# A softmax on one core: the fifth and the sixth chunk are loaded the first time in halves

## The chip, the core and the metric

The kernel runs on one core of a Trainium2 chip. The metric is the device time of one execution in microseconds (us). Three runs of the kernel before took 2488.24 to 2488.63 us, with a median of 2488.45.

## The reference

The kernel computes a softmax over the last axis of float32 logits, 16 x 256 rows of 32768 values each, with a temperature of 1.0:

```python
scaled = logits / temperature
scaled = scaled - scaled.max(axis=-1, keepdims=True)
exp_scaled = np.exp(scaled)
return exp_scaled / exp_scaled.sum(axis=-1, keepdims=True)
```

Every value is read once and written once: 536.87 MB in and 536.87 MB out.

## The kernel before

**Tiling.** The 4096 rows of 32768 values are seen as 8192 half rows of 16384. A group is 128 half rows, one on each partition, that is 64 whole rows; G = 64 groups in all. A group is cut into two chunks of 8192 columns (`_CW`): 128 partitions x 32 KB, 4 MB. So there are 128 chunks. SBUF has six slots of one chunk each (`_BUFS`, 192 KB on every partition); group g has the slots 2g mod 6 and 2g + 1 mod 6 (`slots`). Work is in place: the load, the exponential, the scaling and the store of a chunk all use its slot.

**One group** (class `Half`). For each of its chunks DVE waits for the load and takes the negated maximum of the chunk (`tensor_reduce`, L123); ACT then writes the exponential of the chunk with that maximum as its bias, and sums it as it goes (`activation`, L168). When both are done, DVE swaps the maxima and sums between the two half rows of a row (L134), takes the common maximum (L138), ACT takes the correction factors (L179), DVE sums with them (L142), inverts (L153) and scales each chunk (`tensor_scalar`, L157). Each scaled chunk is stored.

**Who issues what.** SP issues all loads on its own queue (q1 in the profile), and ACT issues the stores (q10) of all groups but the last three, whose stores SP issues behind the last loads (L103). The order of everything is written out by hand; no scheduler is in between.

- SP first issues the loads of the first three groups into the six free slots (L216 to L218). Group 0 is loaded with `load_edge` (L94): each chunk in two halves of 4096 columns (`_EDGE`, 16 KB per partition, 2 MB) with a semaphore each. Groups 1 and 2 are loaded with `load` (L89): one transfer of 4 MB a chunk. The chunks of group 2 are the fifth and the sixth; they go to slots 4 and 5.
- SP then loops 20 times over the six slots (L219 to L222): it waits until the store out of a slot has landed (`st[b]`) and loads the next chunk into it. The last group, number 63, is again loaded in halves (L223 to L225).
- DVE runs group 0 (L228), then a loop of 20 turns of three groups (L229 to L231), whose waits count on the loop's register: `ld[b]` must have reached 16 for each load into slot b, since a transfer adds 16 when it has landed. Groups 61 to 63 follow (L232). ACT has the same structure (L236 to L245).
- Group 63 alone is computed and stored in pieces of 4096 columns; group 0 is loaded in halves and computed in whole chunks.

The counts that DVE waits for stand in these lines:

```python
    def turn(q, i):
        b = slots(q + 1)
        return Half(f"q{q}", (q + 1) % _SETS, b, _CW, lambda c, s: [(ld[b[c]], i * 16)], i)
```

Of the kernel before, what the change touches and what calls it, by code (L numbers as in the profile page):

```python
# [8 lines left out]
_CW = 8192  # L9
_BUFS = 6  # L10
_EDGE = 4096
_SETS = 3
# [13 lines left out]
def kernel(  # L26
# [20 lines left out]
    x = xf.rearrange("n (h v) -> (n h) v", h=2)  # L47
# [20 lines left out]
    ld = [nc.alloc_semaphore(f"ld{b}") for b in range(_BUFS)]  # L68
# [9 lines left out]
    sp, dve, act = nc.sync, nc.vector, nc.scalar  # L78

    def spans(step):  # L80
        return [(s, step) for s in range(0, _CW, step)]

    def xcols(b, s, n):
        return X[:, b * _CW + s : b * _CW + s + n]

    def rows(g):
        return bass.ds(g * P, P)
# [6 lines left out]
    def load_edge(g, c, b):  # L94
        for s, n in spans(_EDGE):
# [3 lines left out]
                out=xcols(b, s, n), in_=x[rows(g), c * _CW + s : c * _CW + s + n]  # L99
            ).then_inc(sem, 16)  # L100

    def store(q, g, c, b, s, n):
        q.dma_start(  # L103
            out=o[rows(g), c * _CW + s : c * _CW + s + n], in_=xcols(b, s, n)
        ).then_inc(st[b], 16)

    class Half:
# [79 lines left out]
        def stores(self, q, g):  # L187
            for k, (c, s, w) in enumerate(self.pieces):
                q.wait_ge(site(self.tag, "sc", k), self.n)
                store(q, g, c, self.slots[c], s, w)  # L190

    def slots(g):
        return [2 * g % _BUFS, (2 * g + 1) % _BUFS]

    def fine(g):
        return lambda c, s: [(edge[g, c, s], 16)]

    def coarse(n16):
        return lambda c, s: [(ld[b], n16)] if s == 0 else []


    def first():
        return Half("f", 0, slots(0), _CW, lambda c, s: [(edge[0, c, p], 16) for p, _ in spans(_EDGE)], 1)

    def turn(q, i):
        b = slots(q + 1)
        return Half(f"q{q}", (q + 1) % _SETS, b, _CW, lambda c, s: [(ld[b[c]], i * 16)], i)

    def last(g):
        b = slots(g)  # L210
        if g == G - 1:
            return Half("l2", g % _SETS, b, _EDGE, fine(g), 1)
        return Half(f"l{g}", g % _SETS, b, _CW, lambda c, s: [(ld[b[c]], (g // _SETS + (b[c] > 1)) * 16)], 1)


    for g in range(_SETS):  # L216
        for c in range(2):
            (load_edge if g == 0 else load)(g, c, slots(g)[c])  # L218
    with sp.Fori(1, turns + 1) as i:  # L219
        for b in range(_BUFS):  # L220
            sp.wait_ge(st[b], i * 16)
# [7 lines left out]
    with dve.Fori(1, turns + 1) as i:  # L229
        for q in range(_SETS):  # L230
            turn(q, i).vector()  # L231
    for g in range(G - 3, G):  # L232
        last(g).vector()


    f = first()  # L236
    f.scalar()
    f.stores(act, 0)
    with act.Fori(1, turns + 1) as i:
        for q in range(_SETS):  # L240
            h = turn(q, i)
            h.scalar()
            h.stores(act, i * _SETS + (q + 1 - _SETS))
    for g in range(G - 3, G):
        last(g).scalar()  # L245


    for g in range(G - 3, G):
        last(g).stores(sp, g)
# [41 lines left out]
```

## Time and profile before

| What | us |
|---|---|
| median of three runs | 2488.45 (2488.24 to 2488.63) |
| the profiled execution | 2488.27 |
| its span, from the first to the last instruction | 2486.5 |
| DVE busy | 1724.6 (69%) |
| ACT busy | 944.5 (38%) |
| POOL busy | 0.2 |

The DMA issues of the page (line, queue, count, KB each, median us from issue to landing):

```profile
xs<-in_logits_dram SPq DMA_DIRECT2D x124, 4096.0 KB, 26.5
out_dram<-xs ACTq DMA_DIRECT2D x122, 4096.0 KB, 48.3
xs<-in_logits_dram SPq DMA_DIRECT2D x8, 2048.0 KB, 16.1
out_dram<-xs SPq DMA_DIRECT2D x4, 4096.0 KB, 33.7
out_dram<-xs SPq DMA_DIRECT2D x4, 2048.0 KB, 21.9
```

The page is read like this. DVE is the vector engine, ACT the scalar engine, SP the engine that only issues here; L90 is line 90 of the kernel. "Busy" counts an engine's own instructions, not the issuing of DMAs. All DMA queues share the core's 16 DMA engines, and a transfer over 128 partitions is spread over all 16. `xs` is the tensor of the six slots. A transfer's time from issue to landing holds its wait in the queue as well as its bytes, and it lands when its last byte has arrived and the semaphore tells so. Times inside the execution are counted from the start of the span. The times to landing of single transfers, which are used below, come from the trace asked for one line in a narrow window; the time of a landing is the time of issue plus that.

### The profile page before, as it was taken

Reading aid. Unit: us, or ns where it says so; the run is one execution under the profiler, and the core shown is the slowest. Engines: PE = TensorE matmul, PEld = TensorE weight load, DVE = VectorE, ACT = ScalarE, POOL = GpSimd, SP = SyncE. Lnnn points to the kernel's source line nnn. Section 1 sums busy time; section 2 is a strip of 40 time slices with the busy share of each in tenths; the row PEclk is TensorE's granted clock in tenths of the full one; section 3 lists DMA queues with packets and bytes.
Section 4 is the critical chain, followed back from the end, with each engine's and each line's share of the span. In section 5 each row is a group of like instructions: output and inputs, shape, how many; then the busy total and the mean of one; then the engine's idle time right before and its main releaser. Section 6 shows DMA issues by size and latency. Waiting matters only on the chain.

```text
span 2486.5 us, 2019 instructions
## 1 busy us (share of the span) xinstructions
DVE 1724.6 (69%) x644; ACT 944.5 (38%) x325; POOL 0.2 (0%) x4
## 2 busy tenths in 40 slices
DVE  6777767767677676676766767667676676766764
ACT  3444333343333433434334343343433434334342
POOL 0000000000000000000000000000000000000000
DMA  9999999999999999999999999999999999999999
GB/s 413 430 435 433 430 438 431 430 438 431 432 436 431 436 432 431 438 430 432 437 430 434 435 430 438 431 430 438 431 432 436 431 436 432 431 438 431 430 437 399
DMA packets 37730, 1073.77 MB, mean 432 GB/s; under 512 B 4192, under 2 KB 4192, under 8 KB 4192
## 3 DMA queue, kind: packets, MB, share of 16 engines
q1 hardware_dynamic: 20160, 562.05, 52.4%
q10 hardware_dynamic: 17568, 511.71, 47.7%
q14 instruction: 2, 0.02, 0.0%
HBM read 536.87 MB, written 536.87 MB: 432 GB/s over the span
## 4 chain that ended last, share of the span: by engine, by line
DMA 58%; DVE 18%; another core or an unknown queue 14%; ACT 8%; issue 1%; SPq 0%; ACTq 0%; DVEq 0%
DMA out_dram<-xs 37%; DMA xs<-in_logits_dram 21%; DVE t L123 11%; ACT xs L168 7%; DVE xs L157 6%; SPq L90 0%; ACT ee L179 0%; DVE t L134 0%; DVE row L153 0%; DVE row L138 0%; DVE junk L142 0%; ACTq L103 0%; SPq L98 0%; DVEq L133 0%
## 5 line engine op out<-in xcount | busy, mean ns | idle before, releaser
L168 ACT ACTIVATE xs<-xs,t 128x8192 f32<-128x8192 f32 (+1 forms) x130 | 912.1, 7016 | 1468.4 <-DVE t L123 1468.4
L123 DVE TENSOR_REDUCE t<-xs 128x1 f32<-128x8192 f32 (+1 forms) x130 | 1110.8, 8551 | 234.0 <-DMA xs<-in_logits_dram 234.0
L157 DVE TENSOR_SCALAR xs<-xs,ee,row 128x8192 f32<-128x8192 f32 (+1 forms) x130 | 576.5, 4478 | 2.3
L134 DVE LOAD_MASK_SELECT t<-t x64 | 0.9, 14 | 470.3 <-ACT xs L168 470.3
L179 ACT ACTIVATE ee<-t,row 128x4 f32<-128x4 f32 x64 | 19.0, 298 | 35.9 <-DVE row L138 35.9
L142 DVE CUSTOM_DVE_ANT_1 junk<-ee,t 128x4 f32<-128x4 f32 x64 | 10.4, 163 | 23.3 <-ACT ee L179 23.3
L168 ACT ACTIVATION_READ_ACCUMULATOR xs<-xs,t 128x1 f32 x130 | 24.3, 187 | 0.0
L153 DVE RECIPROCAL row<-row 128x1 f32<-128x1 f32 x64 | 10.5, 164 | 2.2
L138 DVE TENSOR_REDUCE row<-t 128x1 f32<-128x4 f32 x64 | 10.1, 157 | 2.2
L134 DVE STREAM_SHUFFLE t<-t 128x4 f32<-128x4 f32 x64 | 10.2, 160 | 0.6
L142 DVE DVE_READ_ACCUMULATOR2_ANT row<- 128x1 f32 x64 | 5.3, 82 | 0.0
L168 ACT ACT_TABLE_LOAD x1 | 1.3, 1283 | 0.9 <-SPq L54 0.9
L272 POOL MEMSET const-bfloat16-1.0<- 128x1 bf16 x1 | 0.1, 102 | 0.0
L272 POOL MEMSET const-uint8-127<- 128x1 uint8 x1 | 0.1, 101 | 0.0
L272 POOL MEMSET const-float32-0.0<- 128x1 f32 x1 | 0.1, 99 | 0.2 <-issue 0.2
L272 POOL MEMSET const-float32-1.0<- 128x1 f32 x1 | 0.1, 98 | 0.0
## 6 DMA issues: line engine op xcount, KB each, us to landing
xs<-in_logits_dram SPq DMA_DIRECT2D x124, 4096.0 KB, 26.5
out_dram<-xs ACTq DMA_DIRECT2D x122, 4096.0 KB, 48.3
xs<-in_logits_dram SPq DMA_DIRECT2D x8, 2048.0 KB, 16.1
out_dram<-xs SPq DMA_DIRECT2D x4, 4096.0 KB, 33.7
out_dram<-xs SPq DMA_DIRECT2D x4, 2048.0 KB, 21.9
```

Of the source, the lines that this page charges most:

```text
L123: m = dve.tensor_reduce(out=t[:, k : k + 1], in_=xcols(self.slots[c], s, w), axis=X_, op=A.max, negate=True)
L134: dve.stream_shuffle(out=t[:, 2 * K : 4 * K], in_=t[:, 0 : 2 * K], mask=swap).then_inc(site(tag, "sh"), 1)
L138: dve.tensor_reduce(out=r[:, 0:1], in_=tv[:, :, 0, :], axis=XY, op=A.min).then_inc(site(tag, "mx"), 1)
L142: dve.tensor_tensor_reduce(out=j[:, 0 : 2 * K].rearrange("p (a k) -> p a k", a=2), in0=e[:, 0 : 2 * K].rearrange("p (a k) -> p a k", a=2), ...
L153: dve.reciprocal(out=r[:, 2:3], in_=r[:, 1:2]).then_inc(site(tag, "rc"), 1)
L157: dve.tensor_scalar(out=xs, in0=xs, scalar1=e[:, k : k + 1], scalar2=r[:, 2:3], op0=A.mult, op1=A.mult).then_inc(site(tag, "sc", k), 1)
L168: a = act.activation(out=xs, in_=xs, func=Exp, bias=t[:, k : k + 1], scale=inv_t, accum_out=t[:, K + k : K + k + 1],)
L179: act.activation(out=e[:, 0 : 2 * K].rearrange("p (a k) -> p a k", a=2), in_=tv[:, :, 0, :], func=Exp, bias=r[:, 0:1], scale=-1.0,).then_i ...
L272: nc = _bacc.Bacc("TRN2", target_bir_lowering=False, num_devices=1)
```

## The change

Group 2's two chunks are loaded with a new function, `load_halves`, in two transfers of 4096 columns (16 KB per partition) each. Both halves of a chunk add 16 to the same semaphore `ld[b]`, so slots 4 and 5 now count one transfer more than their chunks, and `landed16` gives the count that DVE waits for: both halves of the first chunk, then one more for each later one. DVE's reduces, their order and all other transfers are the same. An unused function, `coarse`, goes.

```diff
+    def load_halves(g, c, b):
+        for s, n in spans(_EDGE):
+            sp.dma_start(
+                out=xcols(b, s, n), in_=x[rows(g), c * _CW + s : c * _CW + s + n]
+            ).then_inc(ld[b], 16)
+
+
+    def landed16(b, n):
+        return (n + 1) * 16 if b // 2 == _SETS - 1 else n * 16
...
-    def coarse(n16):
-        return lambda c, s: [(ld[b], n16)] if s == 0 else []
-
...
     def turn(q, i):
         b = slots(q + 1)
-        return Half(f"q{q}", (q + 1) % _SETS, b, _CW, lambda c, s: [(ld[b[c]], i * 16)], i)
+        return Half(f"q{q}", (q + 1) % _SETS, b, _CW, lambda c, s: [(ld[b[c]], landed16(b[c], i))], i)
...
-        return Half(f"l{g}", g % _SETS, b, _CW, lambda c, s: [(ld[b[c]], (g // _SETS + (b[c] > 1)) * 16)], 1)
+        return Half(f"l{g}", g % _SETS, b, _CW, lambda c, s: [(ld[b[c]], landed16(b[c], g // _SETS + (b[c] > 1)))], 1)
...
     for g in range(_SETS):
         for c in range(2):
-            (load_edge if g == 0 else load)(g, c, slots(g)[c])
+            (load_edge if g == 0 else load_halves if g == _SETS - 1 else load)(g, c, slots(g)[c])
```

## The prediction

> **What bounds the kernel now.** I read the page's slices and queue rows first, to see whether any engine has idle time that an edit could give back or use up.
>
> ```profile
> DVE  6777767767677676676766767667676676766764
> DMA  9999999999999999999999999999999999999999
> ...
> q1 hardware_dynamic: 20160, 562.05, 52.4%
> q10 hardware_dynamic: 17568, 511.71, 47.7%
> ```
>
> DVE, the busiest engine, works in six to seven tenths of a slice; the 16 DMA engines work in all of them. The packets of the loads' queue (q1) and of ACT's store queue (q10) together fill 100.1% of the span: the transfers follow each other without a gap. Next the same by stretch (columns: length, busy time and count of DVE, ACT, POOL, PE clock, DMA share, GB/s), for the opening, the loop and the last 21.5 us:
>
> ```profile
> 50.00:110.00 60.00, 44.23 (x19) 29.45 (x10) 0.00 (x0) 1.00 0.99 428
> ...
> 400.00:2300.00 1900.00, 1320.44 (x490) 721.97 (x246) 0.00 (x0) 1.00 1.00 433
> ...
> 2465.00:2486.50 21.50, 0.00 (x0) 0.00 (x0) 0.00 (x0) 1.00 0.81 347
> ```
>
> 428 to 433 GB/s at a share of 0.99 to 1.00 in opening and loop; only the very end falls off. The chain of waits gives the price of a transfer: in the loop it repeats a piece each 116.29 us (load issues at 281.54 and 397.83), in which six chunks are loaded and six stored: 116.29 / 12 = **9.69 us for one 4 MB transfer**. 128 loads and 128 stores make 256 x 9.69 = 2480.9 us of the span of 2486.5. The remaining 5.6 are 0.95 to the first issue, 2.3 until its bytes flow (below), 1.2 after the last landing, and about 1.1 that I do not split. So the end is set by bytes in line at the DMA engines, and an edit moves the time only if it makes these engines idle, lets them begin earlier, or makes transfers dearer.
>
> Last, what the engines wait for, and the end of the chain:
>
> ```profile
> DVE t L123 <- DMA xs<-in_logits_dram: 234.0, 58, 13.1
> ```
>
> ```profile
> 2374.95 26.52 DMA xs<-in_logits_dram
> ...
> 2401.50 8.70 DVE t L123
> ...
> 2450.18 9.38 DVE xs L157 x4
> ```
>
> DVE waits for loads 58 times, 234.0 us: in the loop the compute follows the transfers. At the end, the last DVE work starts at 2450.18 and the span goes on to 2486.5 on stores alone.
>
> **The change, part by part.** The profiled execution took 2488.27 us, its span 2486.5, so 1.8 lie around it; the median of the runs is 2488.45, 0.18 more. I add the steps to the profiled time and give the sum against the median.
>
> 1. *Dearer transfers.* The fifth and sixth chunk are 4 transfers instead of 2. The price stands in the opening, where L98 loads halves back to back. Issue times 0.95 and 2.34 with 7.2 and 20.5 us to landing put the first half at 8.15 and the fourth at 22.8: three halves in 14.65, 4.88 each, 9.77 for a chunk. The third and fourth chunk (L90, issued 2.90 and 3.41, landing after 29.6 and 38.8) land 9.7 apart. A split chunk thus costs 0.07 to 0.08 more; twice, **+0.15 us**, all on the path, since the DMA line has no gap. The four half stores at the end agree: from 2470.7 to 2485.3, 4.87 each.
>
>    The other bound: the first half needs 7.2 us to land where one in line takes 4.88, so 2.3 us of a transfer are startup. Shown for both added transfers this is +4.6. I take 0.15, because the added halves are queued at about 4 us and start behind four transfers, as halves two to four of the opening do. 4.6 stays as the range's upper end; no row shows a split chunk coming out cheaper than a whole one.
>
>    The Trainium skill (DMA: Bandwidth & Descriptors, section Anatomy of one DMA) charges each transfer a fixed cost of about 2.0 us on GpSimd's path, which speaks against this change: two more would make an estimate of +4.0. The 4.88 us spacing disagrees for transfers in line; the measurement decides.
>
> 2. *SP's issues.* Two more issues of 0.33 to 0.50 us each (row of L90) put SP's loop about 0.9 us later. SP then waits for the first store, which lands at 68.4 (44.7 + 23.7); the loop is entered near 6. Cost 0; without that cover it would be 0.9, once. Nothing else stands in SP's queue there.
>
> 3. *The waits.* DVE still reduces whole chunks after both halves have landed, so no work begins sooner. In its loop the order of instructions shows one register instruction more (for the count of slots 4 and 5), 20 times. The existing one takes 54 ns (L229), 1.1 us in all, and its sequencer does it beside a TENSOR_SCALAR of 4.5 us. Cost 0; uncovered it would still have to exceed the 3.9 us that DVE waits for loads in each half.
>
> 4. *The share of the two queues in the opening.* This is what really moves. Today the fifth chunk lands at 56.3 (3.95 + 52.4), 14.1 after the fourth (42.2), 4.4 more than 9.7: the first store took those 4.4, so by equal turns sharing began at 47.5. From there each load takes 19.4. How a 16 KB load packet shares with a 32 KB store packet is seen at the end, where L98's first half (issued 2394.2, landing after 18.2, at 2412.4) starts at 2401.5, when the load ahead of it lands (2375.0 + 26.5), beside the last ACT store, which lands at 2410.5 (2350.3 + 60.2). Equal bytes would give it 4.5 of its 4.85 us by then and a landing at 2410.9; equal packets give it a third, 3.0, and 2410.5 + 1.85 = 2412.4. It landed at 2412.4: **turns go by packet**.
>
>    The Trainium skill (DMA: Bandwidth & Descriptors, section Queues, rings and completion order) says that an engine takes its queues in turn, one packet at a time; this trace agrees, with 2412.4 against 2410.9.
>
>    So the fifth chunk's remaining 4.4 us at a third of the engines take 13.2: it lands at 60.7. The first store gets 8.8 of its 9.7 meanwhile, moves the other 0.9 in 1.4, to 62.1, and, with the 1.5 that now lie between its turns' end (66.9) and its landing, lands at 63.6 instead of 68.4. The second store takes 9.7 x 1.5 = 14.6, to 76.7. The sixth chunk has 5.3 by then and the rest alone: it lands at **81.0 instead of 75.7**. The third store is issued by compute at 79.6 as now and finds its queue empty: bytes from 82.4, landing 103.3 instead of 107.1. From there both queues move 32 KB packets: **loads stay about 4 us late, stores about 4 us early**, and nothing pulls them back (98 loads of the loop take 26.5 to 26.6 us to land, without drift). Both waits are cover today. DVE wants the fifth chunk at 83.9 and the sixth at 92.6 (chain: 17.20 us of two reduces from 83.86), 23 and 11.6 us after they land. Bytes moved per us do not change. Cost 0.
>
> 5. *The end.* All 128 loads and ACT's 122 stores stand ahead of SP's last 8 stores, whatever their split. The last group's first store is issued at 2452.62; its predecessor lands at 2465.9 (2427.8 + 38.1). It may be 13.3 - 2.3 (startup) = 11 us later before the DMA engines run dry. Four us late leaves 7. Cost 0; a cover of 0 would cost each us beyond it in full.
>
> Sum: 2488.27 + 0.15 = 2488.4 by the profiled execution, **2488.6 by the median**.
>
> **The rivals.**
> - *Shares go by bytes* (chance 0.05). The sixth chunk still lands near 75.8 and loads keep 26.5. Time 2488.6 all the same; 2412.4 speaks against it.
> - *Startup is shown* (0.04). The engines idle between halves: 2 x 2.3, so 2488.45 + 4.6 = 2493.1, just inside 0.2%. For it: 7.2 against 4.88. Against it: three halves in line without it.
> - *The last stores come too late* (0.04), the slower side. If the loads fall behind by a whole turn of 19.4 us rather than 4, the last group's store is issued at 2472.0, flows from 2474.3, and the engines are dry since 2465.9: 8.4 more, 2488.6 + 8.4 = 2497. It decides from 11 us on. Against it: the third store is issued no earlier than 79.6, and its landing at 103.3 caps the stores' lead at about 4.
> - *Faster* (0.01): only the 2.3 us before the first byte and the 1.2 after the last are free of bytes, and neither is touched.
> - *The change doesn't do what it says*: no chance is kept, since the built order shows two L90 loads fewer and four of 4096 columns in their place on SP.
>
> **How the numbers follow.** The forecast has 0.86. About 0.2% (5.0 us) is what a measurement tells from no change. Same: 0.86 + 0.05 + 0.04 = 0.95; slower 0.04; faster 0.01. The runs before lie 0.4 us apart, so the forecast reaches from 2487.9; the upper end takes in the bound of step 1, 2493.1.
>
> **What would show it.** Step 1: a transfer is 144 packets (128 with data and 16 small ones: 4192 small ones for 262 transfers), so two more make 288 more, 38018 in all. Step 4: the sixth chunk's last half lands near 81, in the loop load to landing rises from 26.5 to about 34.5 and the median store falls from 48.3 to about 40. Step 5: SP's last four stores are issued about 4 us later and the span stays at 2486.6. I am wrong if the DMA share falls under 0.97 over any 50 us between 5 and 2465, or if the spacing of chunk landings in the loop leaves 19.4.

## The result, and the profile after

| What | before | after |
|---|---|---|
| median (us) | 2488.34 (2488.13 to 2488.63) | 2571.72 (2569.31 to 2572.14) |
| ratio, 95% interval | | 1.0333 (1.0321 to 1.0344) |
| profiled execution (us) | 2488.27 | 2572.14 |
| its span (us) | 2486.5 | 2570.4 |

The kernel became 83 us slower. 2488.6 was forecast, with a range to 2493.1. The page of the changed kernel, its parts on DMA:

```profile
DMA  9999999999999999999999999999999999999988
GB/s 409 428 426 424 424 425 422 428 423 421 426 427 425 422 418 426 417 416 423 417 425 414 419 418 414 420 421 418 418 413 418 418 419 423 416 412 421 425 359 371
DMA packets 38018, 1073.78 MB, mean 418 GB/s; under 512 B 4224, under 2 KB 4224, under 8 KB 4224
...
q1 hardware_dynamic: 20448, 562.05, 52.7%
q10 hardware_dynamic: 17568, 511.71, 46.8%
```

The bytes are the same and the packets are the 38018 that were foretold. The DMA engines still look full: nines in all but the last two slices, and 99.5% of the span in the two queues. But the rate is lower from the second slice on: 412 to 428 GB/s, and 359 and 371 in the last two. By stretch (columns as before the change: length, DVE, ACT, POOL, clock, DMA share, GB/s):

```profile
50.00:110.00 60.00, 44.23 (x19) 29.45 (x10) 0.00 (x0) 1.00 1.01 434
110.00:220.00 110.00, 83.69 (x31) 44.18 (x15) 0.00 (x0) 1.00 1.00 423
...
400.00:2300.00 1900.00, 1273.62 (x471) 696.21 (x238) 0.00 (x0) 1.00 1.00 420
```

The second of these stretches before the change:

```profile
110.00:220.00 110.00, 86.36 (x32) 44.18 (x15) 0.00 (x0) 1.00 1.00 434
```

Here the reader sees most of the loss. To 110 us the opening is as good as before. From then on the share is 1.00 as it was, and the rate 420 to 425 instead of 433: the engines don't idle, **they take longer for the same packets**. The trace's packet records say so too: of the packets of 32 KB, 32 of 32000 took over 1.26 us before, 30 of them in the first 100 us; after the change 2536 of 31744 did, in every part of the run. What lies above the usual 1.213 us adds up to 67 us on each of the 16 engines. These packets are not spread evenly. Between 110 and 300 us the records can be sorted onto the 16 engines, since on an engine one packet begins where another ends: of the extra time there, 92% lies in the first three packets that an engine moves of a load, around the end of the store. Summed over the engines this extra time is 61 us; in the same 190 us before the change it is 0.1.

The wait of DVE and the DMA issues answer to the lines shown of before:

```profile
DVE t L133 <- DMA xs<-in_logits_dram: 320.6, 60, 13.3
```

```profile
xs<-in_logits_dram SPq DMA_DIRECT2D x122, 4096.0 KB, 36.9
out_dram<-xs ACTq DMA_DIRECT2D x122, 4096.0 KB, 42.1
```

DVE waits 86.6 us more for loads, three per cent of the span, which is the loss as the compute sees it. A load takes 36.9 us from issue to landing in place of 26.5, a store 42.1 in place of 48.3: loads late, stores early, as foretold.

Where the time went by stage: SP's first load of its loop is issued at 65.3 instead of 68.6 (3.3 us gained), the 120 loads of the loop are issued over 2384.9 us instead of 2306.4 (78.5 lost, 0.66 for each), and from the last of them to the end it is 120.2 us instead of 111.5 (8.7 lost). So the loss is a little at every transfer, not one stall.

**The place of a store against a load.** The chain of waits tells it (columns: start in us, length, what). Before the change:

```profile
979.32 26.53 DMA xs<-in_logits_dram
1027.83 48.29 DMA out_dram<-xs
1095.64 26.54 DMA xs<-in_logits_dram
```

A load lands at 979.32 + 26.53 = 1005.85, a store at 1027.83 + 48.29 = 1076.12. The chain's next load comes six loads later, 1095.64, so a load lands each 19.39 us, and three loads after 1005.85 one lands at 1064.0: the store lands **12.1 us after a load**. After the change:

```profile
1003.76 37.09 DMA xs<-in_logits_dram
1062.83 41.16 DMA out_dram<-xs
1124.98 36.18 DMA xs<-in_logits_dram
```

Loads land at 1040.85 and, six loads later, at 1161.16, that is 20.1 us apart on average, but not evenly. The one issued at 1064.0 takes 37.6 us, so it lands at 1101.6; the store lands at 1103.99, **2.4 us after it**. I call this distance the place of the store in what follows. A landing is that of the last of the 16 engines. For every kernel below the place is given for the landings from 400 to 2300 us, where nothing else is said. In the changed kernel it goes from 4.3 at 150 us to between 2.4 and 4.1.

### The profile page after: what moved, and what is told of

The parts are those of the page before. It is cut to its first block, busy times and chain, and to the rows that moved or that the text cites. A ratio compares the mean times of both kernels' runs of the same rounds, so it can differ in the third digit from the quotient of the medians.

```text
span 2570.4 us, 2041 instructions
## 1 busy us (share of the span) xinstructions
DVE 1724.8 (67%) x644; ACT 944.6 (37%) x325; POOL 0.2 (0%) x4
## 2 busy tenths in 40 slices
DMA packets 38018, 1073.78 MB, mean 418 GB/s; under 512 B 4224, under 2 KB 4224, under 8 KB 4224
## 4 chain that ended last, share of the span: by engine, by line
DMA 61%; another core or an unknown queue 15%; DVE 15%; ACT 7%; issue 1%; SPq 0%; ACTq 0%; DVEq 0%
DMA out_dram<-xs 32%; DMA xs<-in_logits_dram 29%; DVE t L133 9%; ACT xs L178 7%; DVE xs L167 5%; SPq L90 0%; ACT ee L189 0%; DVE t L144 0%; DVE row L163 0%; DVE row L148 0%; DVE junk L152 0%; ACTq L113 0%; SPq L98 0%; DVEq L143 0%
## 6 DMA issues: line engine op xcount, KB each, us to landing
xs<-in_logits_dram SPq DMA_DIRECT2D x122, 4096.0 KB, 36.9
out_dram<-xs ACTq DMA_DIRECT2D x122, 4096.0 KB, 42.1
```

## The experiments

Three theories at first. **A**: the rate hangs on the place of the stores against the loads; the cut chunks only shifted it. **B**: where 16 KB packets meet the first stores, the 16 DMA engines take the store after different packets, and lose a common turn between loads and stores. **C**: the two added transfers, their count or the added register instruction cost.

### Cut chunks that no store meets

```diff
-            (load_edge if g == 0 else load_halves if g == _SETS - 1 else load)(g, c, slots(g)[c])
+            (load_edge if g == 0 else load_halves if g == 1 else load)(g, c, slots(g)[c])
```

The count in `landed16` goes to slots 2 and 3 with it.

> The third and fourth chunk are loaded in halves in place of the fifth and sixth; all else as changed. These halves have moved by 42 us, before the first store at 44.7. If the loss comes from 16 KB load packets beside 32 KB store packets in the opening (theory A or B), the time is that of before, about 2488.6 us, and the loop's loads land after 26.5 us as before. If it comes from the two added transfers, the count or the added register instruction (theory C), the time is about 2571 us again.

Measured: 2488.17 us, 1.000 of before (0.9988 to 1.0011); loads 26.5 us to landing, place 12.1. **C falls**: the same two transfers, counts and register instruction cost nothing that can be measured.

### The first store issued later

The kernel before, with two, four or six dummy activations on ACT between the scaled chunk and its store:

```diff
+    act.wait_ge(site("f", "sc", 0), 1)
+    for k in range(4):
+        act.activation(out=pad[:, 0:1088], in_=xcols(0, 0, 1088), func=Exp, scale=-1.0).then_inc(site("pad"), 1)
+        act.wait_ge(site("pad"), k + 1)
     f.stores(act, 0)
```

> The kernel before; ACT issues the first store about 2.4 us later, after two dummy activations of 1.2 us. No transfer is cut, so all packets beside stores are 32 KB. Theory A (what counts is where in a load transfer the stores begin): store starts two load packets later, it is not known which places are bad; between 2488 and 2571 us. Theory B (the engines lose their common turn only through the mixed packet sizes): 2488.5 us. Theory C: 2488.5 us.

> The same with four dummy activations, about 4.9 us. Then the first store starts beside the second packet of the sixth chunk, so that load and store transfers begin within about 2.4 us of each other, as they do after the change. Theory A: about 2560 to 2571 us without any 16 KB packet. Theory B and C: 2488.5 us.

> The same with six dummy activations, about 7.3 us: the first store starts beside the fourth packet of the sixth chunk. Theory A: nearer to 2488.5 than the run with four, since the ends of loads and stores lie 5 us or more apart again. Theory B and C: 2488.5 us.

Measured: 2490.38 us (1.0006, 0.9995 to 1.0017), 2490.34 (1.0008, 0.9997 to 1.0019) and 2488.39 (1.0002, 0.9991 to 1.0013). Taken alone, the run with four speaks against A. But the place wasn't moved as planned: in the loop it is 14.5, 12.1 and 12.1. With four, the sixth chunk lands at 71.1 and the first store only at 72.3, so the loads' queue runs dry, and the next load begins a fixed time after that store: the old place comes back by itself. A was not tested by this; the one new place that it gives is 14.5, with two dummy activations, and that is as fast as before within 0.2%.

### Loads later, with whole packets only

One or two dummy loads ahead of the third chunk. They have moved before the first store comes; from there on all packets are whole. The lines for two are shown; the tensor `pad` and a wait for these loads at the kernel's end go with them.

```diff
+        for k in range(2 if g == 1 else 0):
+            sp.dma_start(
+                out=pad[:, k * 1920 : (k + 1) * 1920], in_=x[rows(0), k * 1920 : (k + 1) * 1920]
+            ).then_inc(site("pad"), 16)
```

> The kernel before with one dummy load of 128 x 7.5 KB ahead of the third chunk (2.3 us of transfer, done before the first store; its data are not used). Loads are later against the stores and no cut packet meets a store: in the loop a store should land about 12.1 - 4.6 = 7.5 us after a load in place of 12.1. Theory A (the place of stores against loads sets the rate): between 2490.7 and 2571 us. Theory B (the 16 engines lose their common turn where 16 KB packets meet the stores): 2488.4 + 2.3 = 2490.7 us.

> The same with two dummy loads, 4.6 us: in the loop a store should land about 3 us after a load, as it does after the change (2.5 us), with only 32 KB packets beside the stores. Theory A: about 2571 us. Theory B: 2488.4 + 4.6 = 2493 us, and the 16 engines end a load within 3 us of each other to the end.

Measured: with one, 2491.73 us (1.0014, 1.0003 to 1.0025), place 7.3. With two, **2578.32 us** (1.0362, 1.0332 to 1.0392), place 2.4 to 3.9. The stretch from 400 to 2300 us of the kernel with two, and its chain:

```profile
400.00:2300.00 1900.00, 1273.70 (x471) 698.70 (x237) 0.00 (x0) 1.00 1.00 420
```

```profile
1010.94 36.85 DMA xs<-in_logits_dram
1069.78 41.70 DMA out_dram<-xs
1131.57 37.39 DMA xs<-in_logits_dram
```

The reader is to see the changed kernel over again, 420 GB/s at a full share and 36.85 us from load to landing, without one cut chunk beside a store. A load lands at 1047.79, the third after it at 1108.9, the store at 1111.48, 2.6 us later. **This is what A said and B excluded.**

### One of the two cut chunks

```diff
+            (load_edge if g == 0 else load_halves if slots(g)[c] == 4 else load)(g, c, slots(g)[c])
```

(5 in place of 4 for the sixth; `landed16` counts the added transfer for that slot alone.)

> Only the fifth chunk is cut; the first store arrives beside 16 KB packets, as after the change, the sixth chunk has 32 KB packets. Theory B: the engines take the first store after different packets and lose their turn: slow, 2550 to 2571 us. Theory A: loads come only half as late, so a place between before's and after's: between 2488 and 2571 us.

> Only the sixth chunk is cut; the first store arrives beside 32 KB packets, as before. Theory B, if it is the arrival of a store beside small packets that parts the engines: 2488.6 us; if it is the mixing of sizes as such: slow too. Theory A: a place between before's and after's: between 2488 and 2571 us.

Measured: only the fifth cut, **2488.62 us** (1.0003, 0.9991 to 1.0014), place 6.4 at 150 us, 5.4 at 1000, 4.8 at 2300. Only the sixth cut, **2568.67 us** (1.0323, 1.0293 to 1.0353), place about 4 at 150 us, then 2.4 to 3.9. B had it the other way round: the first store meets 16 KB packets in the fast kernel and whole ones in the slow one. The chain and the stretch of the fast kernel:

```profile
976.64 33.15 DMA xs<-in_logits_dram
1031.77 41.57 DMA out_dram<-xs
1092.80 33.23 DMA xs<-in_logits_dram
```

```profile
400.00:2300.00 1900.00, 1320.41 (x490) 722.94 (x246) 0.00 (x0) 1.00 1.00 433
```

Loads 33.15 us to landing, the store at 1073.34 and a load at 1009.79 + 3 x 19.36 = 1067.9: 5.4 us apart, and the full rate.

### The change, made fast again

The changed kernel with the two dummy loads:

> The changed kernel with the two dummy loads of 128 x 7.5 KB ahead of the third chunk: fifth and sixth chunk are still cut, but loads lie another 4.6 us later, so that in the loop a store should land some 13 us after a load (2.5 - 9.1 + 19.4). Theory A (place of stores against loads): fast, 2488.6 + 4.6 = 2493 us. Theory B (cut packets beside stores part the engines): slow, about 2575 us.

Measured: 2494.65 us (1.003, 1.0018 to 1.0042; single times from 2491.86 to 2504.43). Both chunks are cut, and the loss is gone but for the dummy loads' 4.6 us and some scatter. The place came out at 8.4, not at 13.

```profile
400.00:2300.00 1900.00, 1320.37 (x490) 724.04 (x246) 0.00 (x0) 1.00 1.00 433
```

So two dummy loads make the kernel before slow and the changed kernel fast. B is done with.

### Other places

The kernel before with one dummy load of chosen length, into slot 5 ahead of the third chunk; SP waits for it before it issues the sixth chunk's load:

```diff
+        if g == 1:
+            sp.dma_start(out=xcols(5, 0, 6080), in_=x[rows(0), 0:6080]).then_inc(site("pad"), 16)
         for c in range(2):
+            if g == 2 and c == 1:
+                sp.wait_ge(site("pad"), 16)
```

> The kernel before with one dummy load of 128 x 24 KB ahead of the third chunk, 7.2 us (into slot 5, which the sixth chunk's load then fills; SP waits for it first). A store should land about 2.3 us before a load. Theory A1 (two completions close together cost, whichever is first): slow, about 2575 us. Theory A2 (only a store that ends just after a load has begun costs): 2488.4 + 7.2 = 2495.6 us.

> The same with 128 x 20 KB, 6.1 us: loads and stores should land together. Theory A1: slow, about 2575 us. Theory A2: between 2494.5 and 2575 us.

> The kernel before with one dummy load of 128 x 16.5 KB, 4.9 us, ahead of the third chunk: a store should land about 2.3 us after a load, and all packets beside stores are whole. If the order of loads and stores alone is slow: about 2575 us, beginning in the first 200 us while the 16 engines still end a load within 1 us of each other. If engines must be parted first: 2493.3 us.

> The same with 128 x 11.9 KB, 3.6 us: a store should land about 4.9 us after a load. If the slow place ends below 4.9 us: 2492 us. If it reaches over it: about 2575 us.

Measured, in order: 2494.38 us (1.0025, 1.0013 to 1.0036) with place 16.9, that is 2.5 before a load; 2493.08 (1.0024, 1.0012 to 1.0036) with place 0.2; **2577.23** (1.0358, 1.0328 to 1.0388) with place 2.2 in the first turns and 2.4 to 3.8 from 400 us on; 2491.69 (1.0014, 1.0003 to 1.0025) with place 6.4, sliding to 4.8. A1 falls and A2 stands: loads and stores that land together cost nothing, nor does a store that lands 2.5 us before a load. The kernel with 4.9 us shows the onset:

```profile
100.00:200.00 100.00, 72.33 (x30) 36.97 (x13) 0.00 (x0) 1.00 1.00 425
400.00:2300.00 1900.00, 1275.19 (x471) 699.70 (x238) 0.00 (x0) 1.00 1.00 420
```

It is slow from the first turns, at 425 GB/s, while by the semaphore records the first and the last of the 16 engines still end a load 1.0 us apart at 105 us and 2.7 us at 146. So the rate falls before the engines are far apart (15 us at 1000 us). Nor is it enough that they part: in the kernel before with later issues, the last one below, the ends of a load lie 3.9 us apart at 2300 us, at 433 GB/s.

The compute beside the transfers doesn't tell slow from fast either. At 146.1 us a load lands both in the kernel with 4.9 us and in the one with 6.1: in the first DVE began to scale a chunk 1.6 us earlier, in the second 1.7. The first is slow there, the second fast.

### Other rows, another moment of issue

The stores of each group go to the mirrored group of rows; the order and the sizes of the transfers stay:

```diff
-            out=o[rows(g), c * _CW + s : c * _CW + s + n], in_=xcols(b, s, n)
+            out=o[bass.ds((G - 1) * P - g * P, P), c * _CW + s : c * _CW + s + n], in_=xcols(b, s, n)
```

> The changed kernel, but each group's result is stored to the rows of the mirrored group (group 63 - g), so the output has its groups in reverse order. Order and sizes of all transfers stay. If the loss hangs on the order of transfers: about 2571 us again. If it hangs on which rows are read while which are written: another time, down to 2488.6 us.

> The kernel before with the same mirrored stores (output with its groups in reverse order). Order of transfers: 2488.4 us. Rows: any time between 2488.4 and 2575 us.

Measured: 2571.83 us (1.0336, 1.0306 to 1.0366) and 2488.56 us (1.0001, 0.999 to 1.0013). Which group's rows are written while others are read makes no difference.

In the slow place SP also issues a load just after one has begun, 0.2 us after each store's landing. Here GpSimd stands in between and delays the issue by two memsets of 2.5 us:

```diff
-            sp.wait_ge(st[b], i * 16)
+            sp.wait_ge(site("gate", b), i)
...
```

The loop on GpSimd that sets `gate` is left out here.

> The changed kernel; in SP's loop each load is issued some us later than the landing of the store before it: GpSimd waits for the store, does two memsets on an unused tensor, and tells SP. Loads wait 17 us in their queue, so the order of transfers should stay (a store lands 2.4 to 4.5 us after a load). If the moment of SP's issue costs: 2489 us. If the order of the completions costs: about 2571 us.

> The kernel before with the same delay of SP's issues. Loads wait 7.1 us in their queue; if the delay is under that, 2488.4 us by both theories, and the order stays. If it is more, loads start later and the order slides.

Measured: 2561.20 us (1.0292, 1.0262 to 1.0322), place 4.3 at 150 us, then 2.4 to 3.8, loads 31.7 us to landing in place of 36.9. The issue did move, to 3.6 us and more after a store's landing in place of 0.2; the loss stayed but for 10 us. The control took 2489.55 us (1.0004, 0.9993 to 1.0016); its loads slid, as the delay is near the 7.1 us that they wait, to a place of 16.9. The moment of the issue is not the cause.

### All places together

| Kernel | place in the loop (us) | GB/s, 400 to 2300 us | us |
|---|---|---|---|
| loads later by 6.1 | 0.2 | 433 | 2493.08 |
| changed | 2.4 to 4.1 | 420 | 2571.72 |
| changed, issues later | 2.4 to 3.8 | 423 | 2561.20 |
| loads later by 4.9 | 2.4 to 3.8 | 420 | 2577.23 |
| loads later by 2 x 2.3 | 2.4 to 3.9 | 420 | 2578.32 |
| only the sixth cut | 2.4 to 3.9 | 421 | 2568.67 |
| loads later by 3.6 | 6.2 to 4.8 | 433 | 2491.69 |
| only the fifth cut | 6.0 to 4.8 | 433 | 2488.62 |
| loads later by 2.3 | 7.3 | 433 | 2491.73 |
| changed, loads later by 2 x 2.3 | 8.4 to 8.6 | 433 | 2494.65 |
| before | 12.1 | 433 | 2488.34 |
| first store later by 2.4 | 14.5 | 433 | 2490.38 |
| loads later by 7.2 | 16.9 | 433 | 2494.38 |
| before, issues later | 16.5 to 17.0 | 433 | 2489.55 |

The other five repeat a place: about 12.1 at 433 GB/s (third and fourth chunk cut; first store later by 4.9 and by 7.3; before with mirrored stores) and 2.4 to 4.0 at 420 GB/s (changed with mirrored stores).

## Why the prediction was wrong, point by point

**Step 1, dearer transfers (+0.15): right as far as it can be seen.** The kernel with the third and fourth chunk cut stays within 0.1% of before. The bound of 4.6 was never met; neither is the +4.0 estimated from the fixed cost that the Trainium skill gives for GpSimd's path (DMA: Bandwidth & Descriptors, section Anatomy of one DMA).

**Steps 2 and 3, SP's issues and the waits (0): right**, by the same kernel, which has both.

**Step 4, the share in the opening: the mechanism was right, the sizes nearly.** The landings follow from issue plus time to landing in the trace: fifth chunk 60.0 (foretold 60.7), sixth 82.2 (81.0), first store 65.1 (63.6), second store 79.6 (76.7), third store 103.7 (103.3). One reading in it was off, and that the fifth chunk came out so close is in part luck. The sum gives the fifth chunk's 4.4 extra us to the store and lets the sharing begin at 47.5. The packet records of before have the first packet of a store at 49.6, and just ahead of it load packets that took 0.8 us more than usual on each engine. After the change the first packet is at 49.2, and the load packets ahead of it took 1.1 us more. Later sharing and longer packets nearly cancel for the fifth chunk, but not for the stores. The Trainium skill's rule (DMA: Bandwidth & Descriptors, section Queues, rings and completion order), that an engine takes its queues in turn by packets, agrees with the 60.0 in that the turns go by packets and not by bytes. But the page counts some 9 to 17 descriptors to a packet, and here the queues change places after every packet of the records, one row of 16 or 32 KB, of which an engine has eight in a transfer; the records decide. In the loop a load takes 36.9 us (34.5) and a store 42.1 (40).

**The step that failed is the last sentence of step 4: "Bytes moved per us do not change. Cost 0".** It measured +78.5 us over the loop's 120 loads, at 420 GB/s in place of 433. I took 9.69 us a transfer as the engines' price in any order, from a trace that holds one order only: 12.1 us in all of its loop. My own numbers gave the new order: with loads 4 us late and stores 4 early the place goes from 12.1 to 4.1, and 4.3 was measured at 150 us. I wrote the shift down as cover used up, and gave no bound for an order of transfers that the trace doesn't show.

**Step 5, the end: right that the last stores don't come late** (SP's last four are issued from 2539.4 on, while the store ahead lands at 2549.8). The 8.7 us that the end lost lie where engines finish at different times: the 16 ends of the last store are 7.9 us apart, 2.8 before the change, and the share over the last 80.4 us is 0.88, 0.95 before:

```profile
2490.00:2570.40 80.40, 43.98 (x23) 23.02 (x12) 0.00 (x0) 1.00 0.88 370
```

**The rivals.** The slower one had a wrong mechanism: it looked for an engine that idles, and priced it at 2497. None of the others named the rate. Of the signs of being wrong, "the spacing of chunk landings in the loop leaves 19.4" came true: 20.1 on average, while the DMA share did not fall.

**What is shown, and what stays open.** Shown: in this loop the rate falls from 433 to 420 GB/s when a store's last byte lands 2.2 to about 4.5 us after a load's, that is one to two packets into the next load, with the store's packets in between; it does not at 0.2, at a steady 4.8 and above, or at 2.5 before a load. The upper edge is not sharp: single stores of the slow kernels land up to 4.9 us after a load. Cut packets, the two added transfers, the rows written, engines that have already parted and the moment of SP's issue are each excluded as the cause by a run. Open is what inside a DMA engine makes this order dear, and whether places between 0.2 and 2.2 are slow. A candidate, only argued: the Trainium skill (DMA: Bandwidth & Descriptors, section Queues, rings and completion order) states that the semaphore write at a transfer's end lands only after every earlier write of that engine, across its queues; two such writes about two packets apart could hold up what follows. No run here sets those writes apart from the data, and the same distance in the other order (place 16.9) is free, which this alone would not explain.

## What to carry to other kernels

Where two DMA queues keep the engines full, a full share need not be a full rate: read GB/s beside it, and ask in which order the transfers of the two queues end. An edit of the opening can move that order, and a loop in which both queues are always backed up keeps it to the end, so here a few us at the start were worth 3% of the whole. Before pricing such a shift at nothing, look whether the trace holds the new order; if it doesn't, the bound is open, and one dummy transfer of chosen length in the opening is a cheap way to try the places.

## What the runs showed of the hardware

- 128 x 32 KB transfers from two queues moved at 433 or 420 GB/s over 1900 us, with the DMA share at 1.00 in both.
- The load packets just ahead of the kernel's first store are longer: in the kernel before, most engines had two of 1.3 to 2.07 us in place of 1.213 at 46.4 to 49.6 us. 30 of its 32 slow packets lie there. This is not shown of every store that finds its queue empty: the changed kernel's third store does too (the second lands at 79.6, its own first packet moves at 83.6), and the load packets ahead of it take 1.213 us.
- The 16 engines drift even in the fast loop: the first and the last end of a load lie 0.3 us apart at 150 us and 2.6 at 2300 us before the change, without loss. In the changed kernel it is 13 to 18 us from 1000 to 2300 us.
